# A two-layer decoder in one kernel: 32 bytes ahead of the operands, a group of products as its own task, an earlier function table, and two rows on another queue

## The chip, the core and the metric

The kernel runs on one core of a Trainium2 chip. Its engines are TensorE (PE in the rows below, with its weight load as PEld), VectorE (DVE), ScalarE (ACT), GpSimd (POOL) and SyncE (SP), which here only issues DMAs. The metric is the device time of one execution in microseconds (us), lower being better. Before the change the median of three runs is 1519.81 us, from 1519.21 to 1520.61.

## The reference

One sequence of 256 tokens, 1024 wide, goes through two layers and a last RMSNorm, all in float32. Each layer adds four things to the running state `h`:

```python
for l in range(DEPTH):                                   # DEPTH = 2
    h = h + 0.5 * swiglu_ffn(rms_norm(h, norm_g[l, 0]), ffn_w_in[l, 0], ffn_w_out[l, 0])
    u = rms_norm(h, norm_g[l, 1])
    z = u @ mix_w_in[l]                                  # RWKV-7 part, retention part, two gates
    y_a = rwkv7_time_mix(...)                            # a recurrence over the 256 tokens
    y_b = retention_mix(...)                             # chunks of 128 tokens, row b_gn as a gain
    gate_a, gate_b = sigmoid(z's last 2048 columns + mix_gate_b[l])
    h = h + (gate_a * (y_a @ w_branch_a[l]) + gate_b * (y_b @ w_branch_b[l])) @ mix_w_out[l]
    h = h + memory_cross_attn(rms_norm(h, norm_g[l, 2]), mem, ...)
    h = h + 0.5 * swiglu_ffn(rms_norm(h, norm_g[l, 3]), ffn_w_in[l, 1], ffn_w_out[l, 1])
return rms_norm(h, final_norm)
```

The feed-forward parts (FFN) are 2816 wide, the weights of everything are about 260 MB and are read once.

## The kernel before, in words

**Weights.** SyncE's queue brings the weights in the order in which they are used, in pieces of 512 KB, into five buffers `raw`. ScalarE copies each into a rounded form `wh` (line 241), and VectorE subtracts to get the rest `wl` (line 242). There are seven pairs of `wh` and `wl`. The activations are held in the same two parts: `uh` and `ul` (the normalised input, in the pool `up`), and `ah`, `al`, `mTh`, `oTh` and so on (in the 49 working buffers of the pool `ar`). Each product of the reference is then three products on TensorE (`mm3`, which goes by the helper `mm` at line 207): high by high, high by low and low by high. Most have 128 rows, 128 columns of weights in the array and 256 moving columns; a smaller number has 512 moving columns.

**Where things lie.** Pools are laid out one behind the other in the on-chip memory. Counted in bytes within a partition, `wh` and `wl` begin at multiples of 128; the first `uh` and the first working buffer begin 64 bytes past a multiple of 128, and so do all others of these pools, whose buffers are 1 or 2 KB long.

**Order on TensorE.** A planner (`Em`) runs generators as tasks, each with a priority, and keeps its own clock. A task yields a time or an event, and the planner takes the one of best priority that is due. So the order on TensorE is fixed in the program. VectorE, ScalarE and GpSimd follow dependencies and priorities as a scheduler places them; each engine and each DMA queue then works strictly in its own order.

**The mixing stage.** Its main task `mix` computes `z` in column units (`bq`, `bk`, `bv`, `bg`, then the gates). Beside it run `rw_chain` (RWKV-7) and `ret_chain` (retention). In `rw_chain`:
- `scores` fills `U`, which goes to DRAM and comes back as `us`. GpSimd then solves a triangular system in 31 steps, two instructions each (`solve`, lines 1162 and 1167: `tm` from `xs` and `us`, then `xs` from `xs` and `tm`), and sends the result out as `xg` (line 1170). Ahead of the steps stands one product on `xs` (line 1150) whose result nobody reads.
- `late(t)` computes further scores for each half `t` of the tokens: `sc<-qT,beT`, then `sc<-mh,kh` and its companions.
- `inv` zeroes `W` on GpSimd, reads `xg` into it by eight DMAs on SyncE's queue (line 1250), yields `T_W` = 6000 ns, transposes on VectorE to `XQ` (line 1254), and runs small products `iv<-XQ,U` on TensorE. `late(1)` runs before `inv`, in the same task.
- GpSimd also computes reciprocal square roots for the others (`pow_`, line 265: `brn`, `rhf`, `rstd`).

In `ret_g`, GpSimd issues the DMA of a row `gn` (`row`, line 246) for each half of the unit `bg`, and VectorE multiplies by it at line 1406.

**Start and end.** At the start, 20 products of zeros run on TensorE while the first data is on its way; ScalarE loads its function table with its first activation, `uh` (line 414). At the end `acc_last` closes the last FFN product, updates `h`, and calls `final`, which takes the mean square (`stats`), the root, the gain and the output DMAs.

Of the kernel before, what the change touches and what calls it, by code (L numbers as in the profile page):

```python
# [10 lines left out]
F32 = mybir.dt.float32  # L11
# [3 lines left out]
ALU = mybir.AluOpType  # L15
# [3 lines left out]
DFF = 2816  # L19
DEPTH = 2  # L20
CDEC = math.exp(-0.5)
MAGIC = 12582912.0


# [137 lines left out]
class K:  # L162
    NW = 7
    NRAW = 5
    NA = 49
    T_XG, T_W = 57000.0, 6000.0

    def __init__(s, ctx, tc, A):
        s.tc, s.nc, s.A = tc, tc.nc, A
        nc = s.nc  # L170
        ep = ctx.enter_context
        s.em = Em()
        s.pows = []
        s.const = ep(tc.tile_pool(name="const", bufs=1))
        s.rawp = ep(tc.tile_pool(name="raw", bufs=s.NRAW))
        s.wp = ep(tc.tile_pool(name="wp", bufs=s.NW))
        s.sm = ep(tc.tile_pool(name="sm", bufs=2))
        s.up = ep(tc.tile_pool(name="up", bufs=1))
        s.dram = ep(tc.tile_pool(name="dram", bufs=1, space=bass.MemoryType.DRAM))
        s.ar = Slots(ep(tc.tile_pool(name="ar", bufs=1)), s.NA, "a", (P, 512))  # L180
        s.ps = Slots(ep(tc.tile_pool(name="ps", bufs=1, space=bass.MemoryType.PSUM)), 8, "p", (P, 512))
        s.W = Weights(s, s.NW)
        s.setup()
        c = s.const
        s.hT = c.tile([P, 8, 256], F32, name="hT")
        s.gcol = c.tile([P, 112], F32, name="gcol")
        nc.scalar.dma_start(s.gcol, A["gcol"])
        nc.sync.dma_start(s.hT[:, 0:2, :], A["xT"][:, 0:2, :])
        s.ident = c.tile([P, P], F32, name="ident")
        nc.gpsimd.dma_start(s.ident, A["ident"])  # L190
        s.cols = c.tile([P, 8], F32, name="cols")
        nc.gpsimd.dma_start(s.cols, A["cols"])
        s.nhalf = c.tile([P, 8], F32, name="nhalf")
        nc.gpsimd.memset(s.nhalf, -0.5)
        s.ones = c.tile([P, P], F32, name="ones")
        nc.gpsimd.memset(s.ones, 1.0)
        s.onesr = c.tile([P, P], F32R, name="onesr")
        nc.gpsimd.tensor_copy(s.onesr, s.ones)
        s.cumr = c.tile([P, P], F32R, name="cumr")
        s.masks = c.tile([P, 2, P], I32, name="masks")  # L200
        s.gam = c.tile([P, 2, 2, 8], F32, name="gam")
        s.rot = [c.tile([P, 64], F32, name=f"rot{t}") for t in range(2)]
        s.S0 = c.tile([P, 4, P], F32, name="S0")
# [37 lines left out]
        s.nc.scalar.activation(hi, src, AF.Copy)  # L241
        s.nc.vector.tensor_tensor(lo, src, hi.bitcast(F32), ALU.subtract)  # L242

    def row(s, ap, name):
        t = s.ar.alloc(name)
        s.nc.gpsimd.dma_start(t, ap.partition_broadcast(P))
        return t

    def load_w(s, view, n, c):
# [18 lines left out]
    def behind(s, ins, other):  # L268

        s.tc.add_manual_dep(ins.ins, other.ins.name, mybir.DependencyInfo(  # L270
            mybir.DependencyClass.NoSync, mybir.DependencyReason.DATA), reason="behind")

    def stats(s, src, n, eps):
        nc = s.nc
        sq = s.ar.alloc("sq0"), s.ar.alloc("sq1")
        ss = s.sm.tile([P, 2], F32, name="ss", tag="ss")
        for i in range(2):
            nc.scalar.activation(sq[i], src[i], AF.Square, accum_out=ss[:, i:i + 1])
        s.ar.free(*sq)
        x = s.sm.tile([P, 1], F32, name="sx", tag="sx")  # L280
        nc.vector.tensor_tensor(x, ss[:, 0:1], ss[:, 1:2], ALU.add)
        nc.vector.tensor_scalar(x, x, 1.0 / n, eps, ALU.mult, ALU.add)
        r = s.sm.tile([P, 1], F32, name="rstd", tag="rstd")
        s.pow_(r, x, 1)
        return r


    def wcols(s, key, dram, c0, c):
# [85 lines left out]

    def acc_last(s, parts, acc, scale):

        ws = [s.W.next(key) for _, key, _ in parts]
        for t in range(2):
            tok = slice(t * P, (t + 1) * P)
            for n in range(2):  # L380
                cs = slice(n * 512, n * 512 + 512)
                for i, (X, key, k) in enumerate(parts):
                    xh, xl = (x[:, tok] for x in X(k))
                    s.mm3(acc[t][n], xh, xl, ws[i][0][:, 0, cs], ws[i][1][:, 0, cs], False, i == len(parts) - 1)
                with s.tc.high_priority():
                    s.nc.vector.scalar_tensor_tensor(s.h[t][n], acc[t][n], scale[t], s.h[t][n], ALU.mult, ALU.add)
                s.ps.free(acc[t][n])
                yield 0
            s.final(t)


    def new_u(s, l, i):
# [77 lines left out]
    def start(s):  # L470

        nc = s.nc
        with s.tc.manual_schedule(engines={nc.vector.engine, nc.scalar.engine}):

            x = s.ar.alloc("zero", F32R, (P, 256))
            nc.vector.memset(x.bitcast(F32), 0.0)
            b = s.ps.alloc("zero")
            for i in range(20):
                nc.tensor.matmul(b[:, 0:256], x[:, 0:P], x, start=i == 0, stop=i == 19)
            s.ps.free(b)  # L480
            s.ar.free(x)
            for j in range(4):
# [134 lines left out]
        for n in range(2):  # L617
            s.nc.gpsimd.dma_start(s.gain[n], s.A["final_norm"][n * 512:(n + 1) * 512].partition_broadcast(P))

    def final(s, t):  # L620
        nc = s.nc
        with s.tc.high_priority():
            r = s.stats(s.h[t], D, 1e-6)
            o = []
            for n in range(2):
                o.append(s.ar.alloc("o"))
                nc.vector.tensor_tensor(o[n], s.h[t][n], s.gain[n], ALU.mult)
            nc.vector.tensor_scalar(o[0], o[0], r, None, ALU.mult)
            nc.scalar.activation(o[1], o[1], AF.Copy, scale=r)
            for n, q in ((0, nc.sync), (1, nc.scalar)):  # L630
                q.dma_start(s.A["out"][0, t * P:(t + 1) * P, n * 512:n * 512 + 512], o[n])
        s.ar.free(*o)


    def setup(s):
        for l in range(DEPTH):
# [79 lines left out]
    def mix(s, l):  # L716
# [4 lines left out]
        def two():  # L721
            yield from s.psneed(2)
            return [s.ps.alloc("z"), s.ps.alloc("z")]
# [12 lines left out]
            nc.gpsimd.dma_start(s.gam, A["gam"])  # L736
            nc.gpsimd.memset(s.S0, 0.0)
        R = s.R = {"rows": rows}
        for n in ("w", "a", "k", "r", "v", "bq", "bk", "bv", "ya", "yb", "S0", "sol", "gv", "bon", "xg"):
            R["ev_" + n] = Event()  # L740
        em.spawn(s.hp(s.rw_low(l, ps)), 3)
        ps = yield from two()
# [10 lines left out]
        for nm, q in (("bq", 0), ("bk", 1)):  # L753
            ps = yield from two()
            yield from s.unit(X, nm, 8, 512, ps)
            em.spawn(s.ret_rot(nm, q, ps), 4)
        R["bv"] = [[], []]
        for n in range(2):
            ps = yield from two()
            yield from s.unit(X, "bv", 8, 512, ps)  # L760
            s.ret_v(s.evac(ps, "bv"))
        R["ev_bv"].t = em.now + 4150.0
        em.spawn(s.ret_chain(l), 4)
        R["bg"] = [[], []]
        for n in range(2):
            ps = yield from two()
            yield from s.unit(X, "bg", 8, 512, ps)
            s.ret_g(l, n, ps)
# [355 lines left out]
    def rw_chain(s, l):  # L1124
# [8 lines left out]
        for t in range(2):  # L1133
# [6 lines left out]
            for k in range(4):  # L1140
                for q in range(2):
# [5 lines left out]
        xs = s.ar.alloc("xs", F32, (P, 16, 32))  # L1147
        tm = s.ar.alloc("tm", F32, (P, 16, 32))
        nc.gpsimd.dma_start(xs, A["x0"])
        nc.gpsimd.tensor_tensor(tm[:, 0:2, 0:29], xs[:, 0:2, 2:3].broadcast_to([P, 2, 29]),  # L1150
                                xs[:, 2:3, 3:32].broadcast_to([P, 2, 29]), ALU.mult)
        for i in range(2):
            for q in range(2):
                nc.sync.dma_start(us[i][q * 64:(q + 1) * 64], ug[:, 16 * i:16 * i + 16, :])
# [124 lines left out]

        yield from s.psneed(1)  # L1280
        r0 = r_sum(0)
        yield from late(1)
        yield from inv()
        for t in range(2):
            vc = R["v"][t]
            if t:
                yield 3000.0
                yield from s.psneed(1)
            rr = r_sum(1) if t else r0
# [107 lines left out]

    def ret_g(s, l, n, ps):
        nc, R = s.nc, s.R
        gn = s.row(s.A["b_gn"][l, n * 512:(n + 1) * 512], "gn")  # L1400
        for t in range(2):
            th = s.ar.alloc("bg")
            nc.scalar.activation(th, ps[t], AF.Tanh, scale=s.rhf[t])
# [335 lines left out]
```

## Time and profile before

| | us |
|---|---|
| median of three runs | 1519.81 (1519.21 to 1520.61) |
| profiled execution | 1518.1 |
| its span in the trace | 1516.0 |
| TensorE busy in the span | 1495.0, 99% |
| VectorE, ScalarE, GpSimd busy | 1061.9, 760.5, 180.7 |
| DMA | 270.54 MB, mean 178 GB/s |

The profiled execution is one run. Its span is what the trace shows from the first to the last record; 2.1 us of its own time lie around it. A share of busy time is a mean over stages. TensorE's products are pipelined, so a product of 0.28 us is followed by the next one after 0.11 to 0.12 us; what one costs in a run of them is the pitch, the time from one start to the next.

### The profile page before, as it was taken

What the parts mean: (1) busy time and instruction counts of PE and PEld (TensorE: products, weight loads), DVE (VectorE), ACT (ScalarE), POOL (GpSimd) and SP (SyncE); (2) the same over time, 40 slices, a digit from 0 to 9 for tenths busy, and PEclk for the clock granted to TensorE, in tenths of its full rate; (3) what the DMA queues carried; (4) which work ended last, traced back from release to release, by engine and by line L of the source; (5) the groups of instructions that cost most, each with busy time, mean ns of one, the idle gap of its engine ahead of it and who ended that gap; (6) DMA issues with size and microseconds to landing.
All of it is one profiled execution on the core that took longest, in us unless ns stands there. A gap on an engine that the chain in (4) does not pass through costs nothing.

```text
span 1516.0 us, 28626 instructions
## 1 busy us (share of the span) xinstructions
PE 1495.0 (99%) x11754; PEld 1417.9 (94%) x11754; DVE 1061.9 (70%) x1463; ACT 760.5 (50%) x1044; POOL 180.7 (12%) x241
## 2 busy tenths in 40 slices
PE   8999999998999999999999999999999999999997
PEld 8999988788999999999999999887889999999996
DVE  7976699967657757655686666899576577665654
ACT  6554465544434656444455445654454446654442
POOL 3210003272000000000001000224700000000000
PEclk9999999999999999999999999999999999999999
DMA  8776655535546545666568665674364455466651
GB/s 303 228 226 195 195 169 189 152 123 181 168 145 190 170 139 183 191 185 188 173 196 244 195 194 156 193 232 138 95 197 157 156 164 191 126 211 184 189 186 41
DMA packets 137546, 270.54 MB, mean 178 GB/s; under 512 B 18804, under 2 KB 29444, under 8 KB 137416
## 3 DMA queue, kind: packets, MB, share of 16 engines
q1 hardware_dynamic: 133960, 259.94, 55.2%
q0 software_dynamic: 3024, 8.19, 1.9%
q8 instruction: 92, 1.51, 0.4%
q10 hardware_dynamic: 432, 0.58, 0.1%
q14 instruction: 38, 0.31, 0.1%
HBM read 263.31 MB, written 2.23 MB: 175 GB/s over the span
## 4 chain that ended last, share of the span: by engine, by line
PE 83%; DVE 6%; POOL 4%; issue 2%; DMA 2%; ACT 1%; SPq 1%; POOLq 0%; DVEq 0%
PE z L207 21%; PE acc L207 21%; PE u L207 16%; PE g L207 16%; PE xq L207 3%; POOL tm L1162 2%; DVE wl L242 2%; POOL xs L1167 1%; PE tp L219 1%; PE Y L207 1%; PE xo L207 1%; PE xs L207 1%; POOL brn L265 1%; PE SA L207 1%; PE sc L207 1%
## 5 line engine op out<-in xcount | busy, mean ns | idle before, releaser
L242 DVE TENSOR_TENSOR wl<-raw,wh 128x1024 fp32r<-128x1024 f32 (+1 forms) x477 | 580.8, 1224 | 312.7 <-ACT wh L241 310.5
L241 ACT ACTIVATE wh<-raw 128x1024 fp32r<-128x1024 f32 (+1 forms) x477 | 501.2, 1057 | 527.6 <-PE z L207 125.6
L207 PE MATMUL g<-uh,wh 128*128 128x256 f32 x704 | 196.9, 280 | 2.0 <-ACT wh L241 2.0
L207 PE MATMUL g<-uh,wl 128*128 128x256 f32 x704 | 196.7, 279 | 0.9 <-DVE wl L242 0.9
L207 PE MATMUL u<-uh,wh 128*128 128x256 f32 x704 | 196.5, 279 | 0.0
L207 PE MATMUL g<-ul,wh 128*128 128x256 f32 x704 | 196.3, 279 | 0.0
L207 PE MATMUL u<-ul,wh 128*128 128x256 f32 x704 | 195.8, 278 | 0.0
L207 PE MATMUL u<-uh,wl 128*128 128x256 f32 x704 | 195.8, 278 | 0.0
L207 PE MATMUL acc<-ah,wh 128*128 128x256 f32 x528 | 146.9, 278 | 0.0
L207 PE MATMUL acc<-al,wh 128*128 128x256 f32 x528 | 146.6, 278 | 0.0
L207 PE MATMUL acc<-ah,wl 128*128 128x256 f32 x528 | 146.6, 278 | 0.0
L207 PEld LDWEIGHTS g<-uh,wh 128*128 128x128 f32 x704 | 132.9, 189 | 2.4 <-ACT wh L241 2.2
L207 PEld LDWEIGHTS g<-uh,wl 128*128 128x128 f32 x704 | 133.0, 189 | 1.3 <-DVE wl L242 1.3
L207 PEld LDWEIGHTS g<-ul,wh 128*128 128x128 f32 x704 | 132.6, 188 | 0.2
L207 PEld LDWEIGHTS u<-uh,wl 128*128 128x128 f32 x704 | 132.3, 188 | 0.0
L207 PEld LDWEIGHTS u<-uh,wh 128*128 128x128 f32 x704 | 132.2, 188 | 0.0
L207 PEld LDWEIGHTS u<-ul,wh 128*128 128x128 f32 x704 | 131.9, 187 | 0.0
L207 PE MATMUL z<-wh,uh 128*128 128x512 f32 (+1 forms) x320 | 126.6, 396 | 0.0
L207 PE MATMUL z<-wh,ul 128*128 128x512 f32 (+1 forms) x320 | 123.2, 385 | 0.4 <-DVE ul L415 0.4
L207 PE MATMUL z<-wl,uh 128*128 128x512 f32 (+1 forms) x320 | 123.3, 385 | 0.0
L207 PEld LDWEIGHTS acc<-ah,wl 128*128 128x128 f32 x528 | 99.2, 188 | 0.0
L207 PEld LDWEIGHTS acc<-ah,wh 128*128 128x128 f32 x528 | 99.1, 188 | 0.0
(404 smaller groups left out, 3311.9 us busy)
## 6 DMA issues: line engine op xcount, KB each, us to landing
raw<-in_ffn_w_in SPq DMA_DIRECT2D x175, 512.0 KB, 4.1
raw<-in_mix_w_in SPq DMA_DIRECT2D x108, 512.0 KB, 4.4
raw<-in_ffn_w_out SPq DMA_DIRECT2D x88, 512.0 KB, 3.5
raw<-in_cross_w_kv SPq DMA_DIRECT2D x32, 512.0 KB, 3.7
raw<-in_w_branch_b SPq DMA_DIRECT2D x16, 512.0 KB, 4.5
raw<-in_mix_w_out SPq DMA_DIRECT2D x16, 512.0 KB, 3.5
raw<-in_cross_w_q SPq DMA_DIRECT2D x16, 512.0 KB, 3.8
raw<-in_cross_w_o SPq DMA_DIRECT2D x16, 512.0 KB, 4.3
```

What stands on the lines that cost most here:

```text
L207: s.nc.tensor.matmul(out, l, r, start=start, stop=stop)
L219: s.nc.tensor.transpose(out, src, s.ident)
L241: s.nc.scalar.activation(hi, src, AF.Copy)
L242: s.nc.vector.tensor_tensor(lo, src, hi.bitcast(F32), ALU.subtract)
L265: i = s.nc.gpsimd.tensor_tensor(out, src, s.nhalf[:, :n], ALU.pow)
L1162: i = nc.gpsimd.tensor_tensor(tm[:, 0:nr, 0:w], xc, row, ALU.mult)
L1167: nc.gpsimd.tensor_tensor(xs[:, 0:nr, k + 1:32], xs[:, 0:nr, k + 1:32], tm[:, 0:nr, 0:w], ALU.add)
```

## The change

Six edits stand in the diff.

1. `PAD`: a pool of 8 floats (32 bytes) is put ahead of the pools `up` and `ar`. With the new small tile `act0` (64 bytes in its two buffers) the first `uh` and the first working buffer then begin 32 bytes past a multiple of 128. `wh` and `wl` stay at multiples of 128.
2. `late(1)` becomes the task `second()` of its own, of priority 3, which starts 38,000 ns of the planner's clock later; an event `ev_l1` holds back only the second half of the recurrence. `T_W` goes from 6000 to 7500.
3. At the start an activation of one element comes right behind the zeroing of `x`, and 30 products of zeros run in place of 20.
4. The rows `gn` are issued by SyncE, between weights, ahead of the second unit `bv` and the first unit `bg`; `ret_g` takes them from a list.
5. GpSimd's product at line 1150 is dropped.
6. `acc_last` does itself what `final` and `stats` did, with the sum built up as the halves come; the scale 1/n is moved into the square.

```diff
-    T_XG, T_W = 57000.0, 6000.0
+    T_XG, T_W = 57000.0, 7500.0
...
+        pad = ep(tc.tile_pool(name="pad", bufs=1))
         s.up = ep(tc.tile_pool(name="up", bufs=1))
+        pad.tile([P, PAD], F32, name="pad")
...
-    def row(s, ap, name):
+    def row(s, ap, name, q=None):
         t = s.ar.alloc(name)
-        s.nc.gpsimd.dma_start(t, ap.partition_broadcast(P))
+        (q or s.nc.gpsimd).dma_start(t, ap.partition_broadcast(P))
...
+            o = [s.ar.alloc("o") for n in range(2)]
+            ss = s.sm.tile([P, 2], F32, name="ss", tag="ss")
+            x = s.sm.tile([P, 1], F32, name="sx", tag="sx")
...
+                    nc.scalar.activation(sq[:, c0:c1], h, AF.Square, scale=1.0 / 32, accum_out=ss[:, e:e + 1])
+                    s.ar.free(sq)
+                    if e == 0:
+                        nc.vector.tensor_scalar(x, ss[:, 0:1], 1e-6, None, ALU.add)
+                    else:
+                        nc.vector.tensor_tensor(x, x, ss[:, e:e + 1], ALU.add)
+                    nc.vector.tensor_tensor(o[n][:, c0:c1], h, s.gain[n][:, c0:c1], ALU.mult)
...
             nc.vector.memset(x.bitcast(F32), 0.0)
+            nc.scalar.activation(s.sm.tile([P, 1], F32, name="act0", tag="act0"), x[:, 0:1].bitcast(F32), AF.Copy)
             b = s.ps.alloc("zero")
-            for i in range(20):
-                nc.tensor.matmul(b[:, 0:256], x[:, 0:P], x, start=i == 0, stop=i == 19)
+            for i in range(30):
+                nc.tensor.matmul(b[:, 0:256], x[:, 0:P], x, start=i == 0, stop=i == 29)
...
+        R["gn"] = []
+        gn = lambda n: R["gn"].append(s.row(A["b_gn"][l, n * 512:(n + 1) * 512], "gn", nc.sync))
         for n in range(2):
+            if n:
+                gn(0)
             ps = yield from two()
             yield from s.unit(X, "bv", 8, 512, ps)
...
+            if n == 0:
+                gn(1)
             ps = yield from two()
             yield from s.unit(X, "bg", 8, 512, ps)
             s.ret_g(l, n, ps)
...
         nc.gpsimd.dma_start(xs, A["x0"])
-        nc.gpsimd.tensor_tensor(tm[:, 0:2, 0:29], xs[:, 0:2, 2:3].broadcast_to([P, 2, 29]),
-                                xs[:, 2:3, 3:32].broadcast_to([P, 2, 29]), ALU.mult)
...
-        yield from late(1)
+
+        def second():
+            yield 38000.0
+            yield from late(1)
+            R["ev_l1"].t = em.now
+        em.spawn(s.hp(second()), 3)
         yield from inv()
         for t in range(2):
             vc = R["v"][t]
             if t:
+                yield R["ev_l1"]
                 yield 3000.0
...
-        gn = s.row(s.A["b_gn"][l, n * 512:(n + 1) * 512], "gn")
+        gn = R["gn"].pop(0)
```

How the instructions stand at three places, each of before and then of now. Line numbers shift by a few between the two programs; the names are those above.

GpSimd in the first layer's solve, around the rows `gn` (`brn` is retention's reciprocal root, `W` the buffer that is zeroed for `inv`). Before:

```order
L1162 TENSOR_TENSOR tm<-xs,us 128x10x13
L1167 TENSOR_TENSOR xs<-xs,tm 128x10x13
L246 DMA gn<-in_b_gn 128x512 x2
L1246 MEMSET W 128x512
L265 TENSOR_TENSOR brn<-bss,nhalf 128x4
L1162 TENSOR_TENSOR tm<-xs,us 128x10x12
L1167 TENSOR_TENSOR xs<-xs,tm 128x10x12
L1162 TENSOR_TENSOR tm<-xs,us 128x11x11
```

Now:

```order
L1164 TENSOR_TENSOR tm<-xs,us 128x10x13
L1169 TENSOR_TENSOR xs<-xs,tm 128x10x13
L1164 TENSOR_TENSOR tm<-xs,us 128x10x12
L1169 TENSOR_TENSOR xs<-xs,tm 128x10x12
L268 TENSOR_TENSOR brn<-bss,nhalf 128x4
L1164 TENSOR_TENSOR tm<-xs,us 128x11x11
L1248 MEMSET W 128x512
```

The two DMAs of `gn` are gone from GpSimd, and the first `brn` stands one step of the solve later.

TensorE in the first layer, around the first products `iv` (`z<-uh,wh` and its two companions are the gates' products, `tp<-ident,yb` the transposes of retention's result). Before:

```order
L207 MATMUL z<-uh,wh 128x256
L207 MATMUL z<-ul,wh 128x256
L207 MATMUL z<-uh,wl 128x256
L207 MATMUL iv<-XQ,U 32x32 x32
L207 MATMUL z<-uh,wh 128x256
L207 MATMUL z<-ul,wh 128x256
```

Now:

```order
L210 MATMUL z<-uh,wh 128x256
L210 MATMUL z<-ul,wh 128x256
L210 MATMUL z<-uh,wl 128x256
L210 MATMUL iv<-XQ,U 32x32 x32
L222 MATMUL tp<-ident,yb 128x128 x16
L210 MATMUL z<-uh,wh 128x256
L210 MATMUL z<-ul,wh 128x256
```

The `iv` come 12 products of 256 columns later in the stream than before, and the transposes of `yb`, which stood behind 36 such products, follow them at once. The scores of `late(1)`, of which `sc<-qT,beT` stood behind the products `R` and far ahead of `iv`, now stand among these `z`: `sc<-qT,beT` some 120 rows ahead of the first `iv`, the last of the others behind it.

ScalarE at the start (`sq` are the squares for the norm, `gcol` the gains). Before:

```order
L414 ACT_TABLE_LOAD
L414 ACTIVATE uh<-hT,gcol 128x256 x2
L241 ACTIVATE wh<-raw 128x512 x2
L414 ACTIVATE uh<-hT,gcol 128x256 x2
L241 ACTIVATE wh<-raw 128x1024
L414 ACTIVATE uh<-hT,gcol 128x256 x2
L420 ACTIVATE sq<-hT 128x512 x2
L241 ACTIVATE wh<-raw 128x1024
L414 ACTIVATE uh<-hT,gcol 128x256 x2
L420 ACTIVATE sq<-hT 128x512
L241 ACTIVATE wh<-raw 128x1024
```

Now:

```order
L488 ACT_TABLE_LOAD
L488 ACTIVATE act_110<-zero 128x1
L425 ACTIVATE uh<-hT,gcol 128x256 x2
L244 ACTIVATE wh<-raw 128x512
L431 ACTIVATE sq<-hT 128x512
L244 ACTIVATE wh<-raw 128x512
L425 ACTIVATE uh<-hT,gcol 128x256 x2
L431 ACTIVATE sq<-hT 128x512
L244 ACTIVATE wh<-raw 128x1024
L425 ACTIVATE uh<-hT,gcol 128x256 x2
L431 ACTIVATE sq<-hT 128x512
L244 ACTIVATE wh<-raw 128x1024
```

The table load hangs on the zeroing alone, and the squares stand between the first pieces of the weights, where before they came behind the third `uh`.

## Rows read from the trace of the kernel before

**Rows 1.** The page's first part: busy time of each engine, its share of the span, and instructions.

```profile
PE 1495.0 (99%) x11754; PEld 1417.9 (94%) x11754; DVE 1061.9 (70%) x1463; ACT 760.5 (50%) x1044; POOL 180.7 (12%) x241
```

**Rows 2.** The waits of TensorE: what waited, for whom; us in total, times, longest.

```profile
PE iv L207 <- DVE XQ L1254: 7.0, 4, 3.2
...
PE sc L207 <- ACT bqT L1045: 1.7, 2, 0.9
...
PE g L207 <- DVE wl L242: 0.9, 2, 0.6
```

**Rows 3.** Pieces of the chain that ended last, in order of time, from the FFNs and the attention: start, length, and the products that ran without a break. The pitch of a piece is its length by its count.

```profile
44.76 11.31 PE u L207 x96
...
113.22 10.88 PE u L207 x96
...
520.03 2.87 PE xs L207 x24
...
555.67 18.36 PE acc L207 x162
...
1302.15 18.36 PE acc L207 x162
```

**Rows 4.** Two stretches, one inside each of two FFNs: busy us and instructions of each engine, the granted clock of TensorE as a share of full speed, the DMA engines' mean busy share, GB/s.

```profile
590.00:780.00 190.00, 190.00 (x1616) 190.00 (x1615) 120.74 (x138) 88.73 (x104) 0.69 (x1) 1.00 0.62 186
785.00:930.00 145.00, 145.00 (x1282) 145.00 (x1281) 92.20 (x99) 68.99 (x78) 6.74 (x16) 1.00 0.68 206
```

**Rows 5.** Groups of TensorE's products by form, of the many with 256 moving columns and the weights in an operand: count, busy us, mean ns of one (with its passage through the array).

```profile
L207 PE MATMUL g<-uh,wh 128*128 128x256 f32 x704 | 196.9, 280 | 2.0 <-ACT wh L241 2.0
...
L207 PE MATMUL z<-yaTh,wh 128*128 128x256 f32 x64 | 17.9, 279 | 0.0
```

**Rows 6.** The stretches of the mixing stages in which the granted clock of TensorE was at 0.50, the lower of its two levels (1.2 of 2.4 GHz); columns as in rows 4.

```profile
359.30:366.10 6.80, 5.88 (x82) 5.68 (x83) 5.81 (x8) 3.20 (x6) 0.00 (x0) 0.50 0.87 281
...
1048.79:1052.20 3.41, 3.41 (x16) 2.70 (x15) 3.41 (x5) 0.99 (x2) 3.41 (x1) 0.50 0.73 177
...
1106.82:1113.64 6.82, 5.77 (x54) 5.71 (x55) 5.83 (x8) 4.08 (x7) 0.00 (x0) 0.50 0.93 317
```

**Rows 7.** The first full products in each of these stretches, from the timeline of TensorE: start, length, line, output and inputs.

```profile
362.21 0.58 PE L207 MATMUL z<-uh,wh 128*128 128x256 f32 x1
362.59 0.41 PE L207 MATMUL z<-ul,wh 128*128 128x256 f32 x1
362.80 0.42 PE L207 MATMUL z<-uh,wl 128*128 128x256 f32 x1
...
1049.87 0.79 PE L207 MATMUL z<-wh,uh 128*128 128x512 f32 x1
...
1108.86 0.58 PE L207 MATMUL z<-uh,wh 128*128 128x256 f32 x1
```

**Rows 8.** The first layer's chain from the rows `gn` to the products `iv`, from the timeline: start, length, engine; in brackets the engine's idle time ahead of it and what ended that.

```profile
324.91 1.11 POOL L246 DMA_DIRECT2D gn<-in_b_gn  x2
...
328.61 0.75 DVE L1406 SCALAR_TENSOR_TENSOR bg<-bg,rhf,gn 128x512 f32<-128x512 f32 x1 [8.34 <-DMA gn<-in_b_gn]
...
332.52 1.03 POOL L265 TENSOR_TENSOR brn<-bss,nhalf 128x4 f32<-128x4 f32 x1 [5.96 <-DVE bss L1446]
...
351.57 1.73 POOL L1170 DMA_DIRECT2D xg<-xs  x2 [0.30 <-POOL xs L1167]
...
355.75 3.78 SPq L1250 DMA_DIRECT2D W<-xg  x8
...
358.65 0.45 DVE L1254 STREAM_TRANSPOSE XQ<-W 128x256 f32<-128x256 f32 x1 [4.49 <-DMA W<-xg]
...
359.24 1.05 PE L207 MATMUL iv<-XQ,U 32*32 32x32 f32 x32 [3.16 <-DVE XQ L1254]
...
360.72 0.44 DVE L1254 STREAM_TRANSPOSE XQ<-W 128x256 f32<-128x256 f32 x1
```

**Rows 9.** GpSimd's longest instructions, from its timeline: the product of line 1150 in the first layer, and the longest step of the solve in the first and in the second layer.

```profile
249.68 8.37 POOL L1150 TENSOR_TENSOR tm<-xs 128x58 f32<-128x58 f32 x1 [4.17 <-DVE zs L968]
...
297.01 8.50 POOL L1162 TENSOR_TENSOR tm<-xs,us 128x58 f32<-128x58 f32 x1
...
1043.89 8.42 POOL L1167 TENSOR_TENSOR xs<-xs,tm 128x30 f32<-128x30 f32 x1
```

**Rows 10.** The start, from the timeline.

```profile
4.45 1.28 ACT L414 ACT_TABLE_LOAD   x1 [4.45 <-DMA hT<-in_xT]
...
7.23 0.38 PE L207 MATMUL g<-uh,wh 128*128 128x256 f32 x1 [2.02 <-ACT wh L241]
...
9.16 1.06 ACT L241 ACTIVATE wh<-raw 128x1024 fp32r<-128x1024 f32 x1 [0.66 <-DMA raw<-in_ffn_w_in]
```

**Rows 11.** The start, from the chain that ended last: start, length, and what it passed through.

```profile
11.01 1.04 ACT sq L420 x2
...
13.80 0.52 ACT sq L420
...
15.39 0.53 ACT sq L420
...
18.75 2.77 PE g L207 x22
```

**Rows 12.** The end, from the timeline of VectorE: the second small sum.

```profile
1510.15 0.15 DVE L282 TENSOR_SCALAR sx<-sx 128x1 f32<-128x1 f32 x1
```

More of the change, by code (lines that the diff above doesn't have):

```diff
@@ L21 @@
 CDEC = math.exp(-0.5)
+PAD = 8
 MAGIC = 12582912.0
@@ L271, in behind @@
             mybir.DependencyClass.NoSync, mybir.DependencyReason.DATA), reason="behind")
[L273 to L285, printed above, removed]
     def wcols(s, key, dram, c0, c):
@@ L375, in acc_last @@
     def acc_last(s, parts, acc, scale):
+        nc = s.nc
         ws = [s.W.next(key) for _, key, _ in parts]
@@ L379, in acc_last @@
             tok = slice(t * P, (t + 1) * P)
-            for n in range(2):
-                cs = slice(n * 512, n * 512 + 512)
+            o = [s.ar.alloc("o") for n in range(2)]
+            ss = s.sm.tile([P, 2], F32, name="ss", tag="ss")
+            x = s.sm.tile([P, 1], F32, name="sx", tag="sx")
+            ends = (0, 0, 512), (1, 0, 512)
+            for e, (n, c0, c1) in enumerate(ends):
+                cs = slice(n * 512 + c0, n * 512 + c1)
                 for i, (X, key, k) in enumerate(parts):
-                    xh, xl = (x[:, tok] for x in X(k))
-                    s.mm3(acc[t][n], xh, xl, ws[i][0][:, 0, cs], ws[i][1][:, 0, cs], False, i == len(parts) - 1)
+                    xh, xl = (a[:, tok] for a in X(k))
+                    s.mm3(acc[t][n][:, c0:c1], xh, xl, ws[i][0][:, 0, cs], ws[i][1][:, 0, cs], False, i == len(parts) - 1)
                 with s.tc.high_priority():
-                    s.nc.vector.scalar_tensor_tensor(s.h[t][n], acc[t][n], scale[t], s.h[t][n], ALU.mult, ALU.add)
-                s.ps.free(acc[t][n])
-                yield 0
-            s.final(t)
+                    h = s.h[t][n][:, c0:c1]
+                    nc.vector.scalar_tensor_tensor(h, acc[t][n][:, c0:c1], scale[t], h, ALU.mult, ALU.add)
+                    sq = s.ar.alloc("sq")
+                    nc.scalar.activation(sq[:, c0:c1], h, AF.Square, scale=1.0 / 32, accum_out=ss[:, e:e + 1])
[5 more added lines that the diff above has]
+                    nc.vector.tensor_tensor(o[n][:, c0:c1], h, s.gain[n][:, c0:c1], ALU.mult)
+                if c1 == 512:
+                    s.ps.free(acc[t][n])
+                yield 0
+            with s.tc.high_priority():
+                r = s.sm.tile([P, 1], F32, name="rstd", tag="rstd")
+                s.pow_(r, x, 1)
+                nc.vector.tensor_scalar(o[0], o[0], r, None, ALU.mult)
+                nc.scalar.activation(o[1], o[1], AF.Copy, scale=r)
+                for n, q in ((0, nc.sync), (1, nc.scalar)):
+                    q.dma_start(s.A["out"][0, t * P:(t + 1) * P, n * 512:n * 512 + 512], o[n])
+            s.ar.free(*o)
     def new_u(s, l, i):
@@ L618, in h_tok @@
             s.nc.gpsimd.dma_start(s.gain[n], s.A["final_norm"][n * 512:(n + 1) * 512].partition_broadcast(P))
[L620 to L632, printed above, removed]
     def setup(s):
@@ L738, in mix @@
         R = s.R = {"rows": rows}
-        for n in ("w", "a", "k", "r", "v", "bq", "bk", "bv", "ya", "yb", "S0", "sol", "gv", "bon", "xg"):
+        for n in ("w", "a", "k", "r", "v", "bq", "bk", "bv", "ya", "yb", "S0", "sol", "gv", "bon", "xg", "l1"):
             R["ev_" + n] = Event()
```

## The prediction

> **What bounds the kernel now.** I read the engines' totals first: TensorE is busy 99% of the span [rows 1]. So no other engine's work counts unless TensorE waits for it, and there are two places to look: the waits, and what a product costs while nothing waits.
>
> The waits [rows 2] are few: 7.0 us ahead of `iv`, 1.7 ahead of `sc<-qT,beT`, 0.9 for `wl`, and the 2.02 us before the first product [rows 10]. A wait costs more than itself. Behind the waits of the mixing stages the granted clock is at its lower level, 0.50, for 6.80, 3.41 and 6.82 us [rows 6].
>
> The pitch is the larger matter. Products of the same form run at two speeds. At 44.76 us 96 of them take 11.31 us, 117.8 ns each; at 113.22 us 96 take 10.88, 113.3 ns each [rows 3]. Both at a clock of 1.00: in the stretch from 590 to 780 us it is 190 us by 1616 records, 117.6 ns, and from 785 to 930 us 145 by 1282, 113.1 ns [rows 4]. The slow stretch has no more DMA (0.62 against 0.68) and no more work on VectorE (64% of it, and 64% of the other), so load on memory or on VectorE doesn't explain it. Where both operands lie in working buffers, as in `xs`, it is 2.87 us by 24, 119.6 ns [rows 3]. There the two operands start at the same place within 128 bytes; the others read weights at 0 and activations at 64. That the pitch has to do with addresses is thus suggested, not shown: two speeds at one and the same pair of offsets need a second cause besides.
>
> **The change part by part.** The base is the profiled execution, 1518.1 us (its span 1516.0 and 2.1 around it). It lies 1.7 below the median, which is put back at the end.
>
> *Rows `gn` on SyncE's queue, and later `iv`.* The chain in the first layer [rows 8]: GpSimd reaches the issue of `gn` only at 324.91, behind the steps of the solve. VectorE, in order, sits idle 8.34 us until `gn` has landed, so `brn` comes late, and GpSimd idles 5.96 us before it at 332.52. The solve ends that much later: `xg` goes out at 351.57, `W` at 355.75, `XQ` at 358.65 and 360.72, and TensorE has by then waited 3.16 us at 359.24. With `gn` loaded between weights, GpSimd loses the 5.96 us of idle time and the 1.11 of issuing. `xg` goes out at 351.57 - 7.1 = 344.5, `W` 4.2 us later at 348.7, the two `XQ` at 351.6 and 353.7. TensorE came to `iv` at 359.24 - 3.16 = 356.1. Now 12 products stand ahead of it in addition, 1.4 us: 357.5. So the wait goes, with 3.8 us to spare. Less, if TensorE gets there sooner: by 0.9 for the wait that goes at `sc`, by about 1 with a faster pitch; 2 us are left. SyncE's own order holds: its `W` stand behind one weight more than before, which leaves when a `raw` is free, a piece of weights being worth about 2 us of TensorE's time. What could be late next is the third `S`, which VectorE masks between the two `XQ`; nobody on TensorE needs it before the second half of the recurrence. The gain is 7.0 us in both layers.
>
> *Second scores as their own task.* `sc<-qT,beT` waited for `bqT` from ScalarE, 0.9 us in each layer, and now comes some 165 instructions later, when that is long done: 1.7 us. The products that take its place in the order depend on `uh` and weights that are there.
>
> *The clock.* When these waits go, so should the half clock behind them. In it, full products ran from 362.21 to 366.10, 1049.87 to 1052.20 and 1108.86 to 1113.64 [rows 6, 7], together 11.0 us at half speed, so 5.5 are lost. Bounds: 0, if the clock falls at the small products `iv` themselves, and 7.5, half of all busy time in the three rows. I take 5.5, as the fall in the first layer came at 359.30, right behind a wait.
>
> *The start.* The table load at 4.45 is 1.28 long and holds up the first `uh`, and TensorE's first product at 7.23 [rows 10]. With the table in, that product comes some 1.3 us sooner. But TensorE then waits again, at 18.75 for `wl`, and the chain to it passes ScalarE from 9.16 on with squares of 1.04, 0.52 and 0.53 us in it [rows 11]. What counts is how much sooner that `wl` is there. At most all 2.1 us of squares leave the chain; at least 0.3, if the weights' landing sets the pace, which held ScalarE 0.66 us at 9.16 [rows 10]. I take 1.3: one square fits ahead of 9.16, the others only in part. The 30 products of zeros cost nothing, as they end before the weights are there, and the low clock from 7.7 us on, if it goes, is lost in the wait at 18.75.
>
> *The end.* Of the chain behind the last product one instruction of 0.15 us goes [rows 12], and its gap: 0.2 us.
>
> *GpSimd's product on line 1150.* It takes 8.37 us beside VectorE's run of two-input instructions and nobody waits for it [rows 9]: 0. If it were a first use that must be paid once, the 8.37 would now fall to the solve. But the solve pays 8.50 in the first layer in spite of it, and in the second 8.42 in an `xs` that is not even the first of its kind.
>
> So far 7.0 + 1.7 + 5.5 + 1.3 + 0.2 = 15.7: 1502.4.
>
> *The pad.* It touches every product of 256 columns with a weight in it: six groups of 704 (`g`, `u`), three of 528 (`acc`), three of 256, fifteen of 128 and three of 64 [rows 5], 8688 in all. The fast stretches, as the chain's pieces bound them, are 112 to 195, 556 to 587, 781 to 941 and 1302 to 1334 us [rows 3, 4], about 307 us or 2710 products at 113.3. The other 5980 run at 117.8. If offset 32 brings all to 113.3, that is 5980 by 4.5 ns = 26.6 us. If offset 32 is like offset 0, all run at 119.6: 5980 by 1.8 and 2710 by 6.3 ns, 28 us lost. Below, the columns alone at full clock end it: at the low level starts lie 0.21 us apart [rows 7], which is 256 columns at 1.2 GHz (213 ns), and half of that is 106.7. From 113.3 down that would be another 57 us. The row nearest to the new place is that of offset 64, at which the kernel runs now: it is faster than offset 0 in both of its speeds, and the faster of the two exists in it for 300 us at a time. I take 113.3 for all.
>
> A rule speaks against the pad. The Trainium skill, SBUF — State Buffer, "Who interferes with whom", says that TensorE has two read ports, one for the moving operand and one for the weight load, independent of each other, and that it never waits on anyone; by this the place of an operand is worth nothing. TensorE: Matmul & The Clock Gate, "Back-to-back issue gap", gives N/2.4 + 2.5 ns for a single stream, 109.2 for 256 columns. The trace lies above that at each of its three pitches, so something costs 4 to 10 ns a product that this rule doesn't have. By the rule the time would be that of the second case below.
>
> **The rivals.**
> (a) *Forecast*: 1502.4 - 26.6 = 1475.8, and with 1.7 to the median 1477.5. Chance 0.38. Against it: no trace shows offset 32.
> (b) *The pad is worth nothing*: the two speeds come from something that the operands' place doesn't set, such as the moment at which a run of products starts after an interruption; no piece of the chain changes its speed inside a run. Then 1502.4 + 1.7 = 1504, give or take 3. Chance 0.27.
> (c) *The pad does more*: it takes out part of what is left above 106.7 as well, in 256 and 512 columns. A third of the 57 us for the former gives 1458; with as much again from the 512, 1440. Chance 0.11. For it: nothing but the remainder itself.
> (d) *The pad harms*: the weights at 0 and activations at 32 meet as equal offsets do, 119.6 for all: 1502.4 + 28 + 1.7 = 1532. Slower than before it is from a mean pitch 1.8 ns above today's 116.4, that is 118.2. For it: the three pitches don't follow a rule that I can read, and 32 is nearer to 0 than 64 is. Chance 0.13.
> (e) *The wait at `iv` stays*: the 8.4 us of the dropped product fall to the solve, which then ends where it did (7.1 gained, 8.4 lost). The 7.0 us and 4.4 of the clock remain, and with a pad without effect it is 1504 + 11.4 = 1515. Against it: the solve's own 8.5 us in both layers. Chance 0.11, with (b)'s pitch.
>
> **How the numbers follow.** The likeliest is (a), 1477.5. The range takes in (a), (b), half of (c) and of (e): 1440 to 1515, with (d) outside it. (a) alone would be 1472 to 1483, from the bounds of clock and start. A measurement of this kernel can tell about 0.2%, 3 us, from no change. Faster by more: 0.38 + 0.27 + 0.11 and 0.04 of (e), 0.80. Within: 0.05 of (e). Slower: (d) and what is left of (e), 0.15.
>
> **What would show it.** For the pad, pieces of 96 products in the first FFN (34 to 98 us) and the second (590 to 780): 10.88 us each in (a), 11.31 in (b), under 10.8 in (c), 11.48 in (d). For `gn`, no idle time of VectorE at line 1406, GpSimd's `xg` out near 344 us and no wait of TensorE at `iv`; if the step of the solve that takes 8.5 us is followed by a second such step, (e) is right. For the clock, no stretch at 0.50 behind `iv`. For the start, the first product near 5.9 us and the wait for `wl` ending near 17.5. Wrong would be a wait of TensorE that is not among the four of rows 2: `iv`'s second group behind 24 products in place of 36 is where I would look first.

## The result, and the profile after

The changed kernel takes 1531.63 us (median of three, 1531.51 to 1533.73), against 1519.81: a ratio of 1.0082, with a 95% interval from 1.0059 to 1.0105. It is slower by 11.8 us. The forecast was 1477.5. The profiled execution has a span of 1529.8 us, 13.8 more than before.

The engines' totals, as in [rows 1]:

```profile
PE 1505.5 (98%) x11764; PEld 1429.7 (93%) x11764; DVE 1066.9 (70%) x1463; ACT 762.3 (50%) x1045; POOL 162.3 (11%) x235
```

TensorE is still the bound, and it is busy 10.5 us longer with ten products of zeros more, which take 1.7 us (30 take 5.75 now, 20 took 4.02). So most of the loss is in what a product costs. Three stretches, as in [rows 4], the first of them in the fast FFN of before:

```profile
112.00:190.00 78.00, 78.00 (x660) 78.00 (x659) 46.81 (x49) 34.39 (x39) 1.42 (x6) 1.00 0.59 186
590.00:780.00 190.00, 190.00 (x1622) 190.00 (x1621) 120.64 (x137) 89.03 (x105) 0.69 (x1) 1.00 0.59 188
785.00:930.00 145.00, 145.00 (x1238) 145.00 (x1237) 89.12 (x95) 67.17 (x76) 6.23 (x15) 1.00 0.63 200
...
353.67:363.90 10.23, 5.60 (x28) 5.09 (x29) 8.29 (x13) 3.41 (x6) 0.00 (x0) 0.50 0.61 175
1108.00:1118.20 10.20, 6.15 (x30) 5.63 (x31) 8.24 (x14) 3.82 (x6) 0.00 (x0) 0.50 0.63 185
```

The slow stretch of before has become a little faster, 117.1 ns a product in place of 117.6. The fast one is gone: 117.1 in place of 113.1, and from 112 to 190 us 118.2, where before 690 products stood in the same 78 us (113.0). All of it is at full clock, and the two stretches of [rows 4] have less DMA than before. To put a number on it, add the times from the start of each product of 256 columns and 128 rows to the next start, leaving out those of 190 ns and more (half clock, waits): 1034.9 us for 8890 products before, 1046.6 for 8891 now, so 116.4 ns and 117.7 ns in the mean. That is 11.7 of the 13.8 us.

The last two rows are the stretches at half clock. There are two now in the mixing stages, not three, 20.4 us together against 17.0 [rows 6]; TensorE is busy in them for 11.8 us, against 15.1. They lie at new waits:

```profile
PE sc L210 <- DVE S L1125: 13.5, 2, 7.0
PE g L210 <- DVE wl L245: 2.0, 1, 2.0
...
PE g L210 <- ACT wh L244: 0.5, 1, 0.5
```

The waits for `XQ` (7.0) and `bqT` (1.7) [rows 2] are gone, as forecast. In their place TensorE waits 13.5 us for the masks `S` of the second scores. The chain to it in the first layer, from the timeline; the rows answer to [rows 8]:

```profile
300.81 0.23 POOL L1164 TENSOR_TENSOR tm<-xs,us 128x31 f32<-128x31 f32 x1 [21.38 <-DMA us<-ug]
...
344.57 1.16 PE L210 MATMUL sc<-qT,beT 64*128 64x128 f32 x16
...
349.56 1.73 POOL L1172 DMA_DIRECT2D xg<-xs  x2 [0.30 <-POOL xs L1169]
...
354.33 3.78 SPq L1252 DMA_DIRECT2D W<-xg  x8
...
357.20 0.45 DVE L1256 STREAM_TRANSPOSE XQ<-W 128x256 f32<-128x256 f32 x1 [1.88 <-DMA W<-xg]
357.57 1.25 DVE L1125 TENSOR_TENSOR S<-sc,masks 128x512 int32<-128x512 int32 x2
...
358.28 1.18 PE L210 MATMUL sc<-mh,kh 64*128 64x256 f32 x2 [6.99 <-DVE S L1125]
```

The first of these scores are done by 346 us, but in VectorE's order their masks stand behind the transpose `XQ`, and that waits for `W`. Until then VectorE works on what stands ahead of `XQ` (`wl`, `bg`, `yb`) and is idle for 0.91 us at 346.37 and for 1.88 ahead of `XQ`. So the banks of the scores stay full until 358, and the next scores have nowhere to go. The last of the scores stand 72 products ahead of the first `iv` in this trace, not behind it.

At the start:

```profile
1.19 5.75 PE L491 MATMUL zero<-zero 128*128 128x256 f32 x30 [1.19 <-DVE zero L487]
6.77 0.28 PE L210 MATMUL g<-uh,wh 128*128 128x256 f32 x1
...
10.26 2.48 DVE L245 TENSOR_TENSOR wl<-raw,wh 128x1024 fp32r<-128x1024 f32 x1 [1.15 <-ACT wh L244]
10.35 3.52 POOL L436 TENSOR_TENSOR sq<-sq 128x512 f32<-128x512 f32 x2
...
12.79 0.58 PE L210 MATMUL g<-uh,wl 128*128 128x256 f32 x1 [2.01 <-DVE wl L245]
```

The first product comes at 6.77, 0.5 us sooner than before [rows 10], and the 2 us of wait come back at 12.79. The earlier squares bring GpSimd's work on them beside `wl`, which takes 2.48 us there. In `e3_start20` below, with the squares later, the `wl` at this place takes 1.23 us, and GpSimd's work on the squares begins only at 11.96.

### The profile page after: what moved, and what is told of

Same layout as the page of the kernel before. It is cut to its first block, busy times and chain, and to the rows that moved or that the text cites. A ratio compares the mean times of both kernels' runs of the same rounds, so it can differ in the third digit from the quotient of the medians.

```text
span 1529.8 us, 28646 instructions
## 1 busy us (share of the span) xinstructions
PE 1505.5 (98%) x11764; PEld 1429.7 (93%) x11764; DVE 1066.9 (70%) x1463; ACT 762.3 (50%) x1045; POOL 162.3 (11%) x235
## 4 chain that ended last, share of the span: by engine, by line
PE 75%; POOL 3%; DVE 3%; DMA 2%; issue 1%; SPq 0%; ACT 0%; POOLq 0%; DVEq 0%
PE z L210 22%; PE acc L210 18%; PE u L210 12%; PE g L210 12%; PE xq L210 3%; POOL xs L1169 1%; POOL tm L1164 1%; PE tp L222 1%; PE Y L210 1%; DVE wl L245 1%; PE sc L210 1%; PE xo L210 1%; PE xs L210 1%; PE SA L210 1%; DMA raw<-in_mix_w_in 1%
## 5 line engine op out<-in xcount | busy, mean ns | idle before, releaser
L210 PEld LDWEIGHTS acc<-al,wh 128*128 128x128 f32 x528 | 99.3, 188 | 0.0
```

The costliest lines, as they stand in the source:

```text
L210: s.nc.tensor.matmul(out, l, r, start=start, stop=stop)
```

## The experiments

The distances below are from the beginning of the weights `wh`, `wl` to that of `u` and of the working buffers, past a multiple of 256 bytes. Before the change it is 64, now 160 (so 64 and 32 past a multiple of 128).

**1. Another pad, and the second scores put back: four kernels.**

```diff
-PAD = 8
+PAD = 16            # e1_pad64, e1_both
...
-        def second():                       # e1_inline, e1_both
-            yield 38000.0
-            yield from late(1)
-            R["ev_l1"].t = em.now
-        em.spawn(s.hp(second()), 3)
+        yield from late(1)
+        R["ev_l1"].t = em.now
```

`e1_before_pad32` is the kernel before with 24 floats of pad alone.

> The changed kernel with 16 floats of pad in place of 8: u and the working buffers begin 64 bytes past a multiple of 128 again, as before the change. Theory P (the place of the operands sets the pitch): of the 13.8 us that the span grew, 11.7 lie in products of 256 columns (1034.9 us before, 1046.6 now), so these go: about 1520 us, and runs at 113.3 ns come back. Rival Q (the speed comes from where a run of products was interrupted, which the new order changes): unchanged, 1531 us, 117.3 and 118.7 ns. The waits for S stay in both.

> The changed kernel with the second scores inside the main recurrence task again, ahead of the inverse; the pad stays 32. Theory S (the mask of the second scores stands behind the transposes of W in VectorE's order, and TensorE waits for the bank): the 13.5 us of waits for S and most of the 20.5 us at half clock go, the 1.7 us for bqT come back: 1531 - 13.5 - 7 + 1.7, about 1512 us, with 117.3 and 118.7 ns as now. Rival: the late W is the cause, and TensorE then waits for XQ as before the change, 7 to 13 us in all: 1520 to 1530.

> Both edits together: pad 64 and the second scores inside. P and S add: about 1531 - 11.7 - 19 = 1501 us, which would be faster than before. Q with S: 1512. P with the rival of S: 1508 to 1518.

> The kernel before with nothing but a pad (24 floats, since the small tile of the change is not there), which puts u and the working buffers 32 bytes past a multiple of 128. P: 11.7 us slower, about 1531 us, runs at 117.3 and 118.7 ns and none at 113.3. Q: 1520 us and the runs of before, their places in time included.

Measured, each against the kernel before: `e1_pad64` 1499.89 us (0.9871, 0.9856 to 0.9885), `e1_inline` 1549.02 (1.0189, 1.0168 to 1.0210; its runs lie between 1543.6 and 1551.7), `e1_both` 1516.92 (0.9988, 0.9978 to 0.9997), `e1_before_pad32` 1530.18 (1.0069, 1.0052 to 1.0086). The stretches of [rows 4] in `e1_pad64`, with an even larger gain than theory P gave (part 3 says why):

```profile
590.00:780.00 190.00, 190.00 (x1679) 190.00 (x1678) 126.83 (x146) 93.95 (x112) 0.70 (x1) 1.00 0.60 192
785.00:930.00 145.00, 145.00 (x1282) 145.00 (x1281) 90.71 (x100) 67.90 (x79) 6.14 (x15) 1.00 0.64 201
```

The second stretch is as fast as before, and the first has become so too (190 us by 1679, 113.2 ns). In `e1_before_pad32`, one edit to the kernel before:

```profile
785.00:930.00 145.00, 145.00 (x1238) 145.00 (x1238) 89.75 (x95) 66.55 (x76) 6.24 (x15) 1.00 0.63 201
```

It has the 117.1 ns of the changed kernel. So P holds and Q falls: the pad alone makes the kernel before 10.6 us slower. Theory S missed. With the second scores inside, the time rises by 17.4 us:

```profile
PE O L210 <- DVE rS L1125: 28.4, 2, 14.3
```

In that order VectorE reaches `XQ` early, sits idle for `W` (17.74 us in the first layer), and retention's masks `rS` stand behind it. So among the other edits the new task is worth 17 us (at the other distance too: `e1_both` against `e1_pad64`) and is not what made the kernel slower.

**2. Other distances, and the masks ahead of `XQ`.** `e2_pad0` has no pad (128 past 256), `e2_pad96` 24 floats (224); `e2_wp32` moves the weights by 32 bytes and `u` by as much, so that the distance stays 192. `e2_y30` is `e1_pad64` with another start of the task:

```diff
-            yield 38000.0
+            yield 30000.0
```

> The changed kernel without the pad: with the small tile act0 alone, u and the working buffers begin at a multiple of 128, as the weights do. If the offset between the operands sets the pitch, weights with activations behave as the products of two working buffers do, 119.8 ns: 8890 products by 119.8 against 113.3 to 118 at offset 64 give about 1499.9 + 8890 x 5.5 ns = 1549 us. If only offset 32 is bad, 1500.

> The changed kernel with 24 floats of pad: offset 96. If offsets 32 and 96 are alike (the distance to the next multiple of 128 counts, or only the odd multiple of 32 does): 1531 us, 117.3 and 118.7 ns. If what lies behind the weights counts differently from what lies ahead: another pitch, between 1500 and 1550.

> The changed kernel with the weights' pool moved by 32 bytes and u and the working buffers at 96, so that the distance is 64 again while no operand lies on a multiple of 64. If the distance between the operands counts: 1500 us and runs at 113.3 ns. If the place of each by itself counts: 1531 us or more, no run at 113.3.

> Pad 64, and the task of the second scores begins at 30000 in place of 38000, which puts the first two pairs of masks S ahead of the first transpose XQ in VectorE's order. Theory S1 (the order on VectorE is the cause of the wait): no wait of TensorE for S, 14.6 us less, minus what comes back as a wait for XQ, since W lands only at about 349 us and TensorE is then at iv: 3 to 7 us in each layer. In all 1488 to 1499 us. Rival S2 (late W alone is the cause): wait and time unchanged, 1500, named XQ instead of S.

Measured in one run each: `e2_pad0` 1541.65, `e2_pad96` 1538.29, `e2_wp32` 1498.74 us. `e2_y30` in rounds: 1501.47 (0.9880, 0.9863 to 0.9896). The first stretch of [rows 4] in `e2_pad0`, in `e2_pad96` and in `e2_wp32`:

```profile
590.00:780.00 190.00, 190.00 (x1604) 190.00 (x1603) 119.87 (x136) 88.77 (x104) 0.70 (x1) 1.00 0.58 184
```

```profile
590.00:780.00 190.00, 190.00 (x1608) 190.00 (x1607) 120.32 (x136) 88.95 (x104) 0.69 (x1) 1.00 0.58 186
```

```profile
590.00:780.00 190.00, 190.00 (x1678) 190.00 (x1678) 126.95 (x146) 93.70 (x111) 1.32 (x2) 1.00 0.60 192
```

In `e2_wp32` the weights lie where no multiple of 64 is, and it is as fast as `e1_pad64`. So the distance between the operands counts, not the place of either; this is one run, at one distance. The other two missed what was expected of them: 128 is not as slow as two working buffers (118.9 ns in the mean for 119.8), and 224 is not like 160 (118.4 for 117.7).

In `e2_y30` S1 was right about the cause of the wait, and wrong about what its removal brings. The waits for `S` are gone and others have their length (14.1 us for 14.6):

```profile
PE z L210 <- DVE yb L1457: 8.7, 2, 4.4
PE sc L210 <- DVE yb L1457: 3.6, 2, 2.0
PE iv L210 <- DVE ybTl L245: 1.8, 2, 0.9
```

The first two have another cause. `yb` stands well ahead of `XQ` (348.47 here), and VectorE waits there for the root `brn`, which GpSimd computes between the steps of the solve:

```profile
332.33 0.69 DVE L1457 TENSOR_TENSOR yb<-O,brn 128x512 f32<-128x512 f32 x1 [3.79 <-POOL brn L268]
```

**3. 64 and 192, in both kernels; the start; `gn`.** `e1_pad64` differs from the kernel before by more than its five other edits: its distance is 192, not 64. `e4_before192` is the kernel before with 32 floats of pad, `e4_after64` the changed one with no pad and with `act0` in a working buffer, so at 64. `e3_start20` and `e3_gn_pool` are `e1_pad64` with one edit undone each (in `e3_start20` 64 bytes more of pad stand in for `act0`, so the distance stays 192).

```diff
-            for i in range(30):                     # e3_start20, and without act0
+            for i in range(20):
...
-        gn = R["gn"].pop(0)                         # e3_gn_pool, and without the issues by SyncE
+        gn = s.row(s.A["b_gn"][l, n * 512:(n + 1) * 512], "gn")
```

> The kernel before with nothing but 128 bytes of pad (32 floats): the distance from the weights to u and to the working buffers is 192 past a multiple of 256 in place of 64, and still 64 past a multiple of 128. The changed kernel with pad 64 lay at 192 as well, and 7101 of its products went at 113.3 ns, against 2874 of the kernel before. Theory M (the distance modulo 256 decides how often the faster speed is found): about 7000 products at 113.3, 512-column products at 230 ns, 1519.5 - 22, about 1497 us. Rival H (what decides is the order of instructions ahead of a run, which this edit leaves alone): 1519.5 us and the runs of before.

> The changed kernel without the pad and with act0 in a working buffer, so that everything lies exactly where it did before the change (64 past a multiple of 256). All five other edits are in. M: the share of fast products falls back to that of before, about 1500 + 20 = 1520 us, and the five other edits together are worth nothing. H: 1500 us, and they are worth 20.

> The changed kernel with pad 64 (at 192 past 256), its start put back: table load with the first uh, squares later, 20 products of zeros. By the prediction's step on the start it is 1.3 us slower than 1499.9, bounds 0.3 and 2.1. If the start is worth nothing, because TensorE waits for the weights anyway: 1499.9. If the run that follows the start finds another speed: up to 20 us slower.

> The changed kernel with pad 64, the rows gn issued by GpSimd again. By the prediction's step VectorE then waits for gn some 7 to 8 us in each layer, the solve ends 7 us later, and TensorE waits about 14 us more in all, with half the clock behind it: 1515 to 1520. If the wait for gn is hidden: 1500.

Measured: `e4_before192` 1501.03 us (0.9882, 0.9867 to 0.9896), `e4_after64` 1521.03 (1.0010, 1.0000 to 1.0019), `e3_start20` 1499.05 (0.9868, 0.9853 to 0.9882), `e3_gn_pool` 1517.79 (0.9988, 0.9978 to 0.9997). The two stretches in `e4_before192`, then in `e4_after64`:

```profile
590.00:780.00 190.00, 190.00 (x1679) 190.00 (x1678) 127.04 (x146) 93.73 (x112) 0.70 (x1) 1.00 0.60 192
785.00:930.00 145.00, 145.00 (x1282) 145.00 (x1281) 90.71 (x100) 67.90 (x79) 6.13 (x15) 1.00 0.63 201
```

```profile
590.00:780.00 190.00, 190.00 (x1616) 190.00 (x1616) 120.27 (x137) 89.43 (x106) 1.40 (x2) 1.00 0.58 189
785.00:930.00 145.00, 145.00 (x1282) 145.00 (x1281) 93.00 (x100) 69.05 (x78) 6.75 (x16) 1.00 0.66 206
```

M holds in both directions, H falls. 128 bytes of pad are worth 18.8 us to the kernel before. The five other edits together are worth nothing beyond 1.5 us either way: at equal distance the changed program takes 1521.0 for 1519.8 (64), 1531.6 for 1530.2 (160), 1499.9 for 1501.0 (192). The table takes products of 256 columns and 128 rows, start to start, those of 190 ns and more left out; the third column counts those that lie in some 24 in a row with a mean under 114 ns.

| distance past 256 | kernel | in 24 under 114 ns | mean ns | us |
|---|---|---|---|---|
| 64 | before / `e4_after64` | 2869 / 2902 | 116.4 / 116.4 | 1519.8 / 1521.0 |
| 128 | `e2_pad0` | 0 | 118.9 | 1541.7 |
| 160 | `e1_before_pad32` / the changed kernel | 0 / 0 | 117.8 / 117.7 | 1530.2 / 1531.6 |
| 192 | `e4_before192` / `e1_pad64` / `e2_wp32` | 6918 / 7057 / 7144 | 114.4 / 114.3 / 114.3 | 1501.0 / 1499.9 / 1498.7 |
| 224 | `e2_pad96` | 0 | 118.4 | 1538.3 |

The start is worth nothing that these runs can tell: 1499.05 without it, 1499.89 with it. `gn` is worth 18 us, in this order. So each of the two, `gn` on SyncE and the new task, is worth 17 to 18 us as long as the other is in, and with all five edits undone (`e4_before192`) nothing is lost: neither is a gain over the kernel before. With GpSimd issuing `gn`, VectorE waits again and takes the masks `rS` of retention with it:

```profile
PE sc L210 <- DVE rS L1121: 18.6, 2, 9.3
PE sc L210 <- DVE S L1121: 8.5, 3, 4.8
```

```profile
318.94 0.88 DVE L1410 SCALAR_TENSOR_TENSOR bg<-bg,rhf,gn 128x512 f32<-128x512 f32 x1 [11.01 <-DMA gn<-in_b_gn]
```

**4. Other products ahead of the waiting ones.** `e1_pad64` with two numbers changed, in three ways (`e5_y46w14`: 46000 and 14000, `e5_y50w18`: 50000 and 18000, `e5_y30w14`: 30000 and 14000):

```diff
-    T_XG, T_W = 57000.0, 7500.0
+    T_XG, T_W = 57000.0, 14000.0
...
-            yield 38000.0
+            yield 46000.0
```

> Pad 64, the second scores' task 8000 later (46000) and T_W 14000. TensorE then has 72 more full products (8.2 us at 113.3 ns) ahead of the scores that wait for S, and reaches them at about 351.7, when VectorE, behind both XQ (350 and 353), is about to do S; the iv follow 5 us later. Theory L (the wait is a matter of the place in TensorE's order, and there is enough other work to fill it): waits at S of 2 us in each layer in place of 7.2, and less half clock behind them: 1499.9 - 10 - 4, about 1486 us. Rival B (banks and buffers are tied up by what hangs on W, so that work put ahead runs into them and waits there, as with the task at 30000): 1500 us, the same time with another name on the wait.

> The same with 50000 and 18000: 80 to 110 products more ahead of these scores and of iv. L: no wait at S or XQ, 1480 to 1486 us, unless the recurrence that follows now lacks cover behind the gates' products. B: 1500 us.

> The task at 30000 as in the earlier run (1501.5), and T_W 14000: the masks ahead of XQ, the iv 43 products later (4.9 us). L: the waits of 1.8 us at iv go, those for yb (12.3 us) stay, since they lie ahead of it: 1497 to 1500. B: 1500.

Measured: 1497.25 us (0.9854, 0.9839 to 0.9869), 1496.73 (0.9850, 0.9835 to 0.9867) and 1496.85 (0.9851, 0.9835 to 0.9868). That is some 3 us below `e1_pad64` by the medians, with intervals that overlap, and the fastest versions here. L wanted 14 to 20 in the first two. In the third it had 1497 to 1500 and no waits at `iv`, and that came. What TensorE waits for, in the first and in the second:

```profile
PE sc L210 <- DVE thgA L839: 6.6, 4, 3.5
...
PE z L210 <- DVE S L1125: 2.3, 2, 1.2
PE iv L210 <- DVE ybTl L245: 1.9, 2, 0.9
```

```profile
PE tp L222 <- DVE S L1125: 9.9, 2, 5.0
PE sc L210 <- DVE thgA L839: 4.6, 4, 2.1
```

In these two the wait finds other results of VectorE that stand behind `XQ`: gates' (`thgA`) and masks. Not all of it is `W`: in the second, VectorE has both `XQ` done at 352.6 and works on a gate and four `wl` before the masks at 358.50, for which TensorE waits 5.0 us. In the third, as in `e2_y30`, most of the wait is for `yb`, ahead of `XQ`. For the first two B is near: `W` comes when the solve is done, VectorE's order hangs on it, and what TensorE can do meanwhile is limited by banks. That the banks are the limit is argued from these names and from the program, in which a mask empties its bank; no run with more or fewer of them was made.

## Why the prediction was wrong

**The pad: the step that failed.** "I take 113.3 for all", because offset 64 was the nearest row and has that speed for 300 us at a time. Measured at the new distance: no run at 113.3, but 117.3 and 118.7 ns, and 11.7 us lost where 26.6 were to be gained. These 38.3 us are the larger part of the 54.1 between forecast and median. The other 15.8 are as much as all other terms of the sum together (15.7): in sum nothing of them came, and at equal distance the runs say the same. In the sum itself 5980 by 4.5 ns is 26.9, and case (a) by its own bounds is 1474.7 to 1484, not 1472 to 1483; neither changes the outcome. The sign of the pad's term is that of rival (d), though not its size: (d) put 119.6 ns on all and 28 us. Its total, 1532, agrees with the measurement by accident: there the waits were gone.

Two things in the reasoning led there. I wrote of offset 64 that "it is faster than offset 0 in both of its speeds" and took the row nearest in bytes for the nearest in kind. With speeds that jump between 113 and 120 ns and no known rule, neither end was nearer, and (a) and (d) deserved equal chances. And I counted offsets modulo 128; the runs show that 64 and 192, alike there, differ by 2 ns a product.

Against the pad I set a rule of the Trainium skill (SBUF — State Buffer, "Who interferes with whom": TensorE's two read ports are independent, and it never waits on anyone). What I drew from it, that the place of an operand is worth nothing, doesn't hold here: the distance between the two operands alone moves the mean from 114.3 to 118.9 ns. Whether it is the two reads that meet, no run shows. By case (b) the time would have been 1504; it was 1531.63.

**The waits.** The terms 7.0 and 1.7 went as I said, and came back as 13.5 at `S`. The step that failed is "nobody on TensorE needs it before the second half of the recurrence". It looked at who reads the masks, not at what they free: a mask empties the bank of its scores, and the next scores of the same task need one. The sentence also has only the third mask between the two `XQ`; in the trace no mask of this task stands ahead of the first `XQ`, and the first two stand between. With the wait the half clock stayed, so the clock's 5.5 us didn't come either.

The solve itself went as forecast in length: from its first step to `xg` it takes 48.8 us now (300.81 to 349.56), and 56.7 before (294.90 to 351.57), so 7.9 less for a forecast of 7.1. In parts it is luck: GpSimd's idle time ahead of a `brn` fell from 5.96 to 1.24 us and not to nothing, and the solve's one long step took 6.56 us for 8.50, which was not forecast. It also begins 5.9 us later, so `xg` went out at 349.6 and not at 344.5. In `e1_pad64`, with the fast pitch, it begins at 293.2 and `xg` goes out at 342.5; the wait is still 14.6 us, since TensorE is sooner as well. So the pad didn't cause this wait:

```profile
PE sc L210 <- DVE S L1125: 14.6, 2, 7.4
```

**The start.** I took 1.3, bounds 0.3 and 2.1; `e3_start20` gives 0.8 the other way, and nothing within its interval. "The 30 products of zeros cost nothing" was wrong by little: they end at 6.94, and `wh` was there at 6.06. The wait moved to 12.79, which the text foresaw for 18.75.

**The end and line 1150.** The sum goes straight to the root now, as forecast, a small instruction sooner:

```profile
1524.34 0.16 DVE L388 TENSOR_TENSOR sx<-sx,ss 128x1 f32<-128x1 f32 x1
1524.58 0.55 POOL L268 TENSOR_TENSOR rstd<-sx,nhalf 128x1 f32<-128x1 f32 x1 [5.05 <-DVE sx L388]
```

From the last product's start to the span's end it is 7.4 us (1522.37 to 1529.8), and was 8.0 (1507.98 to 1516.0), so 0.6 less for a forecast of 0.2. The dropped product cost nothing: the solve holds one long step as before, of 6.56 us, and is shorter as a whole. Rival (e) falls.

## What to carry to other kernels

Where a stream of products has no waits and still two speeds, move one operand by steps of 32 bytes and time each; here 128 bytes of pad alone took 1.2% off the kernel before, and 96 bytes put 0.7% on. Which distances are the faster ones, 64 and 192 here, is known for this shape and layout alone. An edit that also moves buffers must be timed at equal places, or its own effect can't be told from theirs. And when an instruction is put behind a wait on an engine that works in order, list what each result behind it frees, not only who reads it.

## What the runs showed of the hardware that was not expected

- The pitch of products of 256 columns with rounded float32 operands depends on the distance between weights and moving data: 113.3 ns for four in five of them at 192 bytes past a multiple of 256, for a third at 64, for none at 128, 160 and 224. That it repeats every 256 bytes is not shown: no distance was taken twice, 256 apart. At distance 0 (`xs`, `xo`, both operands in working buffers) the mean is 119.6 to 119.9 ns in all these programs. Products of 512 columns with a pitch of 225 to 245 ns share it in part: 230.1 ns in the mean at 192, 232.4 at 128, 233.2 at 64 and 224, 233.4 at 160.
- At every distance but 224, where 118.2 ns is nearly all, there are two or more speeds, each stable for tens of microseconds. The two programs at 64 have 2869 and 2902 products at the faster one, at the same places of the FFNs, though their mixing stages differ. At 192 the places are others, and not everything is faster: 96 products `g` of the second FFN that take 10.88 us at 574.03 in the kernel before take 11.31 at 569.31 in `e4_before192`.
- The speed can change inside a stream that nothing interrupts. It does so at some of the few products `rb` (of a diagonal and of ones), here in the kernel before from 113.3 to 117.9 ns, and in `e4_before192` from 117.7 to 113.8:

```profile
584.91 2.72 PE u L207 x24
587.63 0.45 PE rb L207 x4
588.07 5.66 PE u L207 x48
```

```profile
583.89 5.65 PE u L210 x48
589.54 0.24 PE rb L210 x2
589.78 2.73 PE u L210 x24
```

What in them picks the speed is open; no run here addressed it.
